# Token scale of the mixer heads on DVE, sparse heads spread over two products, reloads on POOL's queue

## The chip, the cores and the metric

The kernel runs on one core of a Trainium2 chip. The metric is the device time of one execution in microseconds (us), and a kernel's time is the median over its runs.

## The reference

One layer of a hybrid decoder block, for one sequence of 512 tokens with a width of 2048, all in f32. The part that matters here is the mixer: eight heads of forgetting attention (FoX, group A) and eight heads of sparse attention (NSA, group B), each group normalised over its 1024 columns, scaled, and multiplied with `w_out`:

```python
o_f = _fox_attention(fh(q_f), fh(k_f), fh(v_f), log_f)
o_n = _nsa_attention(nq(q_n), nkv(k_c), nkv(v_c), nkv(k_s), nkv(v_s), nkv(k_w), nkv(v_w),
                     gates, positions, cmp_pos, w_kc1, w_kc2, w_vc1, w_vc2)
y_f = _rmsnorm(o_f.reshape(B, S, FOX_HEADS * HEAD_DIM), beta_fox)
y_n = _rmsnorm(o_n.reshape(B, S, NSA_HEADS * HEAD_DIM), beta_nsa)
return jnp.concatenate([y_f, y_n], axis=-1) @ w_out
```

Ahead of it stand the modulation by `c @ w_ada`, a norm and the projection `u @ w_in`; behind it a residual, a second norm, a SwiGLU feed-forward layer and the final norm.

## The kernel before, in words

**Products.** Activations lie transposed, 128 columns by 512 tokens in a tile. Each f32 product is made of three matmuls on values cut to a high and a low half (high x high, low x high, high x low). `gemm` (L287) goes over the contraction in chunks of 256 rows: SP loads a raw chunk (L225, tag `wr`, 3 buffers), ACT copies the high half (L244), DVE subtracts to get the low half (L249), and PE multiplies. The halves have 2 buffers (`wh`, `wl`), and every third chunk uses a spare pair (`wx`).

**Order of work.** SP's queue is kept in the order in which the program is written (L109). In the attention stage the other engines' orders are made by the compiler's scheduler, in which what stands earlier in the program comes first where both are ready; from L1244 on all orders are as written. The attention runs as a list of steps (score, flip, value product) of which `gemm` takes some per chunk (`n_att`, L301). Other side work, the modulation blocks `side_ada` (L373) and the sparse heads' mixing `side_mix`, are generators advanced by `pump` (L365), some steps per chunk.

**Stage around the change.** A loop over four pairs of FoX heads (L986) makes q and k (L988) and then v (L999) of a pair, each with its own `gemm`, while attention steps of earlier heads run. v's product has 8 chunks of 24 matmuls of 256 columns. Each finished head is copied from PSUM (L864, tag `sc`), stored to DRAM (`osp`, L865, ACT's queue), squared (L871) and the square added on POOL (L875). When all eight heads of a group are there, the sums over columns (L882) give each token's scale 1/rms, which `rows_of` (L172) spreads into a tile of rows with 8 matmuls (L175) and a copy on ACT (L177): `rbn` for the sparse group, `rbf` for FoX.

**Mixing.** `reload` (L966) brings a head back from DRAM into a tile of tag `sc`, which has five buffers and which the attention's probabilities `p`, the head's copy `o` and its square `sq` use as well. `mix_chunk` (L959) multiplies it by the token scale (L960; on DVE for FoX heads 0, 2, 4, 6, on POOL for the rest), scales it by beta into the high half of `y` on ACT (L962), and makes the low half on DVE (L963).

**The sparse heads** are mixed by `mix_nsa` (L971): its first step makes `rbn`, each further step reloads and mixes one head (8 to 15). `mix_hook` (L982) pumps it in v's product of the last pair: one step in chunk 1, two in each chunk after, so that all heads are through with chunk 5. What might be left is pumped at L1023.

**`w_out`** follows (L1030). Its rows are taken in the order of `order`: heads 8 to 15 (sparse) first, then 0 to 7 (FoX). The first group `g0` has four banks and stops after the sparse heads (4 chunks of 512 columns, 24 matmuls of 512 columns each, L1031), with the last two FoX heads' attention beside it. Then the attention is drained (L1032), the FoX scale rows are made (L1033), and the second group `g1` (two banks, 4 chunks of 256 columns, 12 matmuls each, L1041) runs over the sparse heads, while `fox_hook` (L1036) reloads and mixes two FoX heads per chunk. The FoX halves of `g0` and `g1` come in the loop of L1205, then the remaining columns of `w_out`, with the residual (L1076), whose results POOL's queue stores (L1234).

Of the kernel before, what the change touches and what calls it, by code (L numbers as in the profile page):

```python
# [13 lines left out]
OP = mybir.AluOpType  # L14
# [9 lines left out]
FH = 8  # L24
# [55 lines left out]
def hymba_block(ctx: ExitStack, tc: tile.TileContext, x, c, positions, w_ada, b_ada, norm_attn,  # L80
                norm_ffn, w_in, b_fgate, cmp_pos, w_kc1, w_kc2, w_vc1, w_vc2, beta_fox, beta_nsa,
                w_out, w_gate, w_up, w_down, final_norm, cst, out):
    nc = tc.nc
# [18 lines left out]
    def uid(s):  # L102
        n_uid[0] += 1
        return f"{s}_{n_uid[0]}"
# [9 lines left out]
    def split_ap(t):  # L114
        return t.bitcast(F32)
# [56 lines left out]
    def rows_of(r, tag, s):  # L172
        b = bank(tag)
        for t in range(NT):
            nc.tensor.matmul(b[:, t * P:(t + 1) * P], r[:, t:t + 1].to_broadcast([P, P]), ident,  # L175
                             start=True, stop=True)
        nc.scalar.copy(s, b)  # L177
        return s
# [5 lines left out]
    for t in range(NT):  # L184
        for g in range(4):
            src = xtok[t, g // 2][:, g % 2, :]
# [30 lines left out]
    def load_w(parts, ct, nk=2, extra=None, src=None, width=T, bufs=3):  # L217
        return fetch_w(parts, ct, nk, extra, src, width, bufs)()
# [68 lines left out]
    def gemm(parts, a, nchunk, outs, extra=None, order=None, n_ada=0, n_cmp=0, n_att=0, k0=0, k1=None,  # L287
             hook=None, start=0, first=()):
        order = list(range(nchunk)) if order is None else order
        for ct in range(k0 // 2, (nchunk if k1 is None else k1) // 2):  # L290
            i = ct - k0 // 2
            wh, wl = first[i]() if i < len(first) else load_w(parts, order[2 * ct] // 2, extra=extra)
            pump(side_ada, n_ada)
            pump(side_cmp, n_cmp if ct > 1 else ct)
            pieces = [x for o in outs for x in bank_pieces(o)]
            for n, piece in enumerate(pieces):
                for k in range(2):
                    i = ct * 2 + k
                    piece(wh, wl, k, a[order[i]], i == start, i == nchunk - 1)
                if 2 * n + 2 in (len(pieces) - len(pieces) % 2, 2 * len(pieces)):  # L300
                    att.run(n_att)  # L301
            if hook is not None:
                hook(ct)
# [5 lines left out]
    def bank_pieces(out):  # L309
        kind, w0, n, b = out  # L310

        def ws(wh, wl, k, ahl, first, last):
            mm_ws(b, wh, wl, k, w0, *ahl, first, last)

        def tok(t):
            ts = slice(t * P, (t + 1) * P)

            def f(wh, wl, k, ahl, first, last):
                ah, al = ahl[0][:, ts], ahl[1][:, ts]
                if kind == "as":  # L320
                    mm_as(b[t][:, 0:n], wh[:, k, w0:w0 + n], wl[:, k, w0:w0 + n], ah, al, first, last)
                else:
                    pick = [v[:, k, 0:3 * P].rearrange("p (a b) -> p a b", b=P)[:, 0::2, :]
                            if kind == "as02" else v[:, k, w0:w0 + n] for v in (wh, wl)]
                    mm_as(b[t // 2][:, t % 2, :], pick[0], pick[1], ah, al,
                          first and t % 2 == 0, last, skip_group_check=True)
            return f

        return [ws] if kind == "ws" else [tok(t) for t in range(NT)]
# [35 lines left out]
    def pump(side, n):  # L365
        while n and side:
            try:
                next(side[0])
                n -= 1
            except StopIteration:  # L370
                side.pop(0)
# [31 lines left out]
    def act_tile(name, i):  # L403
        h = act.tile([P, T], F32R, tag="ah", name=uid(name + "h"), bufs=ND)
        l = act.tile([P, T], F32R, tag="al", name=uid(name + "l"), bufs=ND)
        return h, l
# [100 lines left out]
    while step < SLOTS + 8 or todo:  # L507
# [9 lines left out]
        i = {7: 0, 0: 1, 1: 2}.get(r, 3)  # L517
# [4 lines left out]
        i = AT.get(r, 3) if j < NJ else AT_END.get(r, 3)  # L522
# [44 lines left out]
        if n is not None:  # L567
            jj = n // 8
            for k2, sec in ((0, 1), (1, 0)):
                m0 = sec * ND + 2 * jj  # L570
                nc.vector.tensor_tensor(mod[:, m0:m0 + 2], sums[jj][:, 2 * k2:2 * k2 + 2], b_mod[:, m0:m0 + 2],
                                        op=OP.add)
# [38 lines left out]
    def sc_tile(name):  # L611
        return pa.tile([P, T], F32, tag="sc", name=uid(name), bufs=5)
# [45 lines left out]
    def q_tmp(name):  # L658
        return pa.tile([P, T], F32, tag="qh", name=uid(name), bufs=6)
# [144 lines left out]
    osp = dram.tile([FH + NH, P, T], F32, name="osp")  # L804
# [73 lines left out]
    def sum_rstd(tiles, n, tag, name, b=None):  # L878
        b = bank(tag) if b is None else b
        for i, a in enumerate(tiles):  # L880
            for t in range(NT):
                nc.tensor.matmul(b[:, t:t + 1], a[:, t * P:(t + 1) * P], one_col, start=i == 0 and t == 0,  # L882
                                 stop=i == len(tiles) - 1, skip_group_check=True)
        return rstd_of(b[:, 0:NT], n, name)
# [72 lines left out]
    y = {}  # L957

    def mix_chunk(src, i, rb):  # L959
        (nc.gpsimd if i >= FH or i % 2 else nc.vector).tensor_tensor(src, src, rb, op=OP.mult)  # L960
        h, l = act_tile("y", i)
        nc.scalar.activation(h, src, AF.Copy, scale=beta[:, i:i + 1])  # L962
        nc.vector.scalar_tensor_tensor(l, src, beta[:, i:i + 1], split_ap(h), op0=OP.mult, op1=OP.subtract)  # L963
        y[i] = (h, l)

    def reload(i):  # L966
        o = sc_tile("or")
        nc.sync.dma_start(o, osp[i])
        return o

    def mix_nsa():  # L971
        while "r" not in rs_n:
            yield
        rb = rows_of(rs_n["r"], "s", q_tmp("rbn"))
        yield
        for h in range(NH):
            mix_chunk(reload(8 + h), 8 + h, rb)
            yield

    side_mix = [mix_nsa()]  # L980

    def mix_hook(ct):  # L982
        if ct >= 1:
            pump(side_mix, 1 if ct == 1 else 2)

    for pr in range(4):  # L986
        Z = [bank("mm") for _ in range(4)]
# [4 lines left out]
        for i in range(2):  # L992
# [7 lines left out]
             hook=mix_hook if pr == 3 else None, first=w_vf)  # L1000
# [19 lines left out]

    while "r" not in rs_n:
        att.step()
    pump(side_mix, 1000)  # L1023

    def out_group(i0, n, tags):
        Z = [bank(t) for t in tags[:n]]
        return [cols(w_out, i0 * P, n * P)], y, ND, [("ws", m * P, P, Z[m]) for m in range(n)]

    order = list(range(8, 16)) + list(range(8))
    g0 = out_group(0, 4, BANKS_A)  # L1030
    gemm(*g0, order=order, n_ada=1, n_att=1.25, k1=8)  # L1031
    att.drain()  # L1032
    rb = rows_of(sum_rstd(osum[0], FH * HD, "o", "rsf"), "o", q_tmp("rbf"))  # L1033
    fox = order[8:]

    def fox_hook(ct):  # L1036
        for h in fox[2 * ct:2 * ct + 2]:
            mix_chunk(reload(h), h, rb)
# [239 lines left out]
    rb = ps2.tile([P, T], F32, tag="y", name=uid("py"), bufs=8)  # L1278
# [11 lines left out]
    for s in range(S):  # L1290
# [20 lines left out]
        n, i = divmod(s - A0, 4)  # L1311
# [66 lines left out]
    for p, ph in enumerate(phases):  # L1378
# [3 lines left out]
        for g in range(4):  # L1382
            Z = banks4()

            def hook(ct):
                if p == 0 and ct == 2:
                    for i in range(4 * g, 4 * g + 4):
                        nc.sync.dma_start(hT[i], hsd[i])
                if p == 3 and g == 3 and ct == 2:
                    fsum["b"] = bank("o")  # L1390
                    sum_tok(fsum, fsum["t"], True, False)
                if nxt and (ct % 2 or nk < 12):
                    b.append(h_tile(nxt.pop(0)))

            gemm([cols(w_down[P * ph[0]:], 512 * g, 512)], a, nk, [("ws", m * P, P, Z[m]) for m in range(4)],
                 hook=hook, first=w_first if p == 0 and g == 0 else ())
# [42 lines left out]
```

## Time and profile before

| what | value |
|---|---|
| median of 3 runs | 2440.64 us (2437.82 to 2442.27) |
| the profiled execution | 2438.08 us |
| its span, first to last instruction | 2436.3 us |
| mean granted clock of TensorE | 0.977 |
| busy share of PE, DVE, ACT, POOL | 96%, 65%, 42%, 14% |
| reloads of heads (L968) | 16 of 256 KB, from SP's queue |

PE is the matrix engine, DVE the vector engine, ACT the scalar engine, POOL the GpSimd engine; SP only sends transfers. A matmul's row shows a duration longer than the distance to the next, since matmuls are pipelined; the distances of the starts give the rate. The granted clock is a share of full speed: 1.00 is 2.4 GHz and 0.50 is 1.2 GHz. In a row of a timeline, what stands in brackets is the idle time of the engine just before and what ended it. In a row that merges several instructions (x2), the duration runs from the first one's start to the last one's end, waits between them included. SPq is SP's queue. A row of busy time by stretch has the stretch, its length, then the busy us and the instructions (x) of PE, of PE's weight loads, of DVE, ACT and POOL, then the granted clock, the busy share of the DMA engines and GB/s.

### The profile page before, as it was taken

Reading aid. Unit: us, or ns where it says so; the run is one execution under the profiler, and the core shown is the slowest. Engines: PE = TensorE matmul, PEld = TensorE weight load, DVE = VectorE, ACT = ScalarE, POOL = GpSimd, SP = SyncE. Lnnn points to the kernel's source line nnn. Section 1 sums busy time; section 2 is a strip of 40 time slices with the busy share of each in tenths; the row PEclk is TensorE's granted clock in tenths of the full one; section 3 lists DMA queues with packets and bytes.
Section 4 is the critical chain, followed back from the end, with each engine's and each line's share of the span. In section 5 each row is a group of like instructions: output and inputs, shape, how many; then the busy total and the mean of one; then the engine's idle time right before and its main releaser. Section 6 shows DMA issues by size and latency. Waiting matters only on the chain.

```text
span 2436.3 us, 38417 instructions
## 1 busy us (share of the span) xinstructions
PE 2349.1 (96%) x14677; PEld 2100.5 (86%) x14677; DVE 1583.2 (65%) x2719; ACT 1026.5 (42%) x1544; POOL 341.2 (14%) x370
## 2 busy tenths in 40 slices
PE   6998999999999999889999999999999999999998
PEld 4777887888887777789999999999999888888887
DVE  7867887787655566596777677777676633333333
ACT  3335444334323323365555555555555422222233
POOL 0002002000102021251222221212121100000010
PEclk8999999999999999899999999999999999999998
DMA  9974643453563287469898889988988644333322
GB/s 331 322 232 143 178 142 101 122 180 119 164 181 122 82 274 255 159 145 231 214 230 220 221 217 229 224 219 219 216 200 196 187 156 141 121 117 122 105 94 99
DMA packets 322713, 440.31 MB, mean 181 GB/s; under 512 B 26224, under 2 KB 217552, under 8 KB 322528
## 3 DMA queue, kind: packets, MB, share of 16 engines
q1 hardware_dynamic: 289104, 348.21, 44.3%
q0 software_dynamic: 31120, 85.45, 18.9%
q10 hardware_dynamic: 2304, 4.20, 0.5%
q8 instruction: 115, 1.88, 0.3%
q14 instruction: 70, 0.57, 0.1%
HBM read 340.18 MB, written 28.38 MB: 151 GB/s over the span
## 4 chain that ended last, share of the span: by engine, by line
PE 55%; DVE 1%; DMA 0%; issue 0%; ACT 0%; SPq 0%; DVEq 0%; ACTq 0%
PE py L1173 12%; PE py L1176 11%; PE py L1175 11%; PE psmm L278 3%; PE psmm L280 3%; PE psmm L279 3%; PE pss L278 2%; PE pss L279 2%; PE pss L280 2%; PE pso L278 1%; PE pso L279 1%; PE pso L280 1%; DMA wr<-in_w_down_dram 0%; PE pso L1070 0%; DVE ul L1153 0%
## 5 line engine op out<-in xcount | busy, mean ns | idle before, releaser
L249 DVE TENSOR_TENSOR wl<-wr,wh 128x1024 fp32r<-128x1024 f32 (+2 forms) x211 | 238.8, 1132 | 371.1 <-ACT wh L244 369.5
L244 ACT CAST wh<-wr 128x1024 fp32r<-128x1024 f32 (+2 forms) x211 | 199.7, 948 | 528.9 <-PE psmm L279 204.0
L1176 PE MATMUL py<-uh,ls 128*128 128x256 f32 x1408 | 398.4, 283 | 2.8 <-DVE ls L1119 2.8
L1173 PE MATMUL py<-uh,hs 128*128 128x256 f32 x1408 | 399.3, 284 | 0.9 <-DVE ev L1190 0.5
L1175 PE MATMUL py<-ul,hs 128*128 128x256 f32 x1408 | 398.4, 283 | 1.8 <-DVE ul L1153 1.8
L1113 ACT CAST hs<-sum 128x1024 fp32r<-128x1024 f32 x176 | 184.6, 1049 | 377.0 <-PE py L1175 256.6
L1119 DVE TENSOR_TENSOR ls<-sum,hs 128x1024 fp32r<-128x1024 f32 x176 | 215.3, 1223 | 196.3 <-ACT hs L1113 196.3
L1175 PE MATMUL py<-ul,hx 128*128 128x256 f32 x1056 | 298.7, 283 | 4.1 <-DVE ul L1153 4.1
L1173 PE MATMUL py<-uh,hx 128*128 128x256 f32 x1056 | 299.3, 283 | 1.7 <-ACT uh L1152 1.4
L1176 PE MATMUL py<-uh,lx 128*128 128x256 f32 x1056 | 298.3, 282 | 0.0
L1176 PEld LDWEIGHTS py<-uh,ls 128*128 128x128 f32 x1408 | 268.0, 190 | 3.6 <-DVE ls L1119 3.6
L1173 PEld LDWEIGHTS py<-uh,hs 128*128 128x128 f32 x1408 | 268.1, 190 | 2.7 <-DVE ev L1190 1.3
L1175 PEld LDWEIGHTS py<-ul,hs 128*128 128x128 f32 x1408 | 268.0, 190 | 2.7 <-DVE ul L1153 2.7
L1109 POOL DMA_DIRECT2D lx<-raw x176 | 156.1, 887 | 579.2 <-ACT lx L1108 431.8
L1175 PEld LDWEIGHTS py<-ul,hx 128*128 128x128 f32 x1056 | 200.8, 190 | 4.9 <-DVE ul L1153 4.8
L1173 PEld LDWEIGHTS py<-uh,hx 128*128 128x128 f32 x1056 | 200.6, 190 | 2.2 <-ACT uh L1152 1.7
L1176 PEld LDWEIGHTS py<-uh,lx 128*128 128x128 f32 x1056 | 200.6, 190 | 0.0
L386 DVE SCALAR_TENSOR_TENSOR acc<-ad,sl,acc 128x512 f32<-128x512 f32 x180 | 143.2, 796 | 41.7 <-DMA ad<-in_w_ada_dram 40.1
L1108 ACT ACTIVATE lx<-raw 128x768 fp32r<-128x768 f32 x176 | 148.0, 841 | 1.8 <-DMA raw<-in_w_gate_dram 1.8
L1104 ACT CAST hx<-raw 128x768 fp32r<-128x768 f32 x176 | 144.4, 820 | 9.0 <-DMA raw<-in_w_gate_dram 9.0
L278 PE MATMUL psmm<-fh,wh 128*128 128x512 f32 x352 | 137.0, 389 | 0.0
L280 PE MATMUL psmm<-fh,wl 128*128 128x512 f32 x352 | 136.9, 389 | 0.0
(442 smaller groups left out, 5290.4 us busy)
## 6 DMA issues: line engine op xcount, KB each, us to landing
lx<-raw POOLq DMA_DIRECT2D x176, 384.0 KB, 5.2
ad<-in_w_ada_dram SPq DMA_DIRECT2D x128, 512.0 KB, 3.9
raw<-in_w_up_dram SPq DMA_DIRECT2D x176, 256.0 KB, 4.1
raw<-in_w_gate_dram SPq DMA_DIRECT2D x176, 256.0 KB, 4.4
wr<-in_w_down_dram SPq DMA_DIRECT2D x88, 512.0 KB, 3.7
ad<-in_w_ada_dram SPq DMA_DIRECT2D x128, 256.0 KB, 6.0
wr<-in_w_in_dram SPq DMA_DIRECT2D x104, 256.0 KB, 3.4
wr<-in_w_in_dram SPq DMA_DIRECT2D x24, 512.0 KB, 4.9
```

The costliest lines, as they stand in the source:

```text
L244: nc.scalar.copy(wh[:, :, sc], v)
L249: nc.vector.tensor_tensor(held[1][:, :, sc], v, split_ap(held[0])[:, :, sc], op=OP.subtract)
L278: nc.tensor.matmul(dst, wh[:, k, w], ah, start=first, stop=False)
L279: nc.tensor.matmul(dst, wh[:, k, w], al, start=False, stop=False)
L280: nc.tensor.matmul(dst, wl[:, k, w], ah, start=False, stop=last)
L1108: nc.scalar.activation(lx[s], raw[s][:, 1:4, :], AF.Copy, scale=-1.0)
L1109: nc.gpsimd.dma_start(split_ap(lx[s]), raw[s][:, 1:4, :], accum_op=OP.add)
L1113: nc.scalar.copy(hs[s], sums[s])
L1119: nc.vector.tensor_tensor(ls[s], sums[s], split_ap(hs[s]), op=OP.subtract)
L1173: nc.tensor.matmul(o, wh[:, wi, js], vh[:, vi, :], start=k == 0 and j == 0, stop=False, skip_group_check=True)
L1175: nc.tensor.matmul(o, wh[:, wi, js], vl[:, vi, :], start=False, stop=False, skip_group_check=True)
L1176: nc.tensor.matmul(o, wl[:, wi, js], vh[:, vi, :], start=False, stop=k == KG - 1, skip_group_check=True)
```

## The change

All token-scale multiplies go to DVE. The reloads are issued on POOL's queue instead of SP's. In v's product of the last pair each chunk from the second on takes one step of the sparse mixing (rows in chunk 1, heads 8 to 13 in chunks 2 to 7), head 14 follows behind the loop, and head 15 goes into the first chunk of `w_out`'s first group; `while len(y) < 2` has nothing to do there, and the later chunks' pumps find the generator ended.

```diff
@@ -957,7 +957,7 @@
     def mix_chunk(src, i, rb):
-        (nc.gpsimd if i >= FH or i % 2 else nc.vector).tensor_tensor(src, src, rb, op=OP.mult)
+        nc.vector.tensor_tensor(src, src, rb, op=OP.mult)
         h, l = act_tile("y", i)
@@ -965,7 +965,7 @@
     def reload(i):
         o = sc_tile("or")
-        nc.sync.dma_start(o, osp[i])
+        nc.gpsimd.dma_start(o, osp[i])
         return o
@@ -981,7 +981,7 @@
     def mix_hook(ct):
         if ct >= 1:
-            pump(side_mix, 1 if ct == 1 else 2)
+            pump(side_mix, 1)
@@ -1020,7 +1020,9 @@
     while "r" not in rs_n:
         att.step()
-    pump(side_mix, 1000)
+    pump(side_mix, 1)
+    while len(y) < 2:
+        pump(side_mix, 1)
@@ -1028,7 +1030,7 @@
     g0 = out_group(0, 4, BANKS_A)
-    gemm(*g0, order=order, n_ada=1, n_att=1.25, k1=8)
+    gemm(*g0, order=order, n_ada=1, n_att=1.25, k1=8, hook=lambda ct: pump(side_mix, 2 if ct < 2 else 1000))
     att.drain()
```

## Rows read from the trace of the kernel before

**Rows 1.** The page, part 1: busy time and share of the span, TensorE

```profile
PE 2349.1 (96%) x14677; PEld 2100.5 (86%) x14677; DVE 1583.2 (65%) x2719; ACT 1026.5 (42%) x1544; POOL 341.2 (14%) x370
```

**Rows 2.** Busy time by stretch, 771 to 880 us

```profile
771.00:803.00 32.00, 27.16 (x212) 26.65 (x211) 18.22 (x20) 13.29 (x20) 12.67 (x8) 0.95 0.37 116
803.00:840.00 37.00, 37.00 (x178) 29.17 (x177) 17.77 (x45) 12.37 (x31) 1.30 (x1) 1.00 0.13 43
840.00:860.00 20.00, 16.70 (x69) 12.50 (x68) 13.18 (x20) 10.05 (x16) 6.48 (x4) 0.83 0.51 173
860.00:880.00 20.00, 20.00 (x89) 16.13 (x88) 12.56 (x16) 5.16 (x7) 0.39 (x1) 1.00 0.71 236
```

**Rows 3.** Timeline of PE, value product of the last head pair (start, duration)

```profile
786.94 0.28 PE L284 MATMUL psmm<-wh,ul 128*128 128x256 f32 x1
787.06 0.28 PE L285 MATMUL psmm<-wl,uh 128*128 128x256 f32 x1
790.05 0.39 PE L283 MATMUL psmm<-wh,uh 128*128 128x256 f32 x1 [2.71 <-ACT wh L244]
...
792.68 0.58 PE L285 MATMUL psmm<-wl,uh 128*128 128x256 f32 x1 [2.13 <-DVE wl L249]
...
795.61 0.28 PE L283 MATMUL psmm<-wh,uh 128*128 128x256 f32 x1
...
802.45 0.40 PE L278 MATMUL psmm<-yh,wh 128*128 128x512 f32 x1
```

**Rows 4.** Timeline of SP's queue, reloads (L968) and weight loads (L225)

```profile
767.40 15.45 SPq L968 DMA_DIRECT2D or<-osp  x2
782.90 0.43 SPq L225 DMA_DIRECT2D wr<-in_w_in_dram  x1
...
831.96 1.95 SPq L968 DMA_DIRECT2D or<-osp  x2
834.00 0.39 SPq L225 DMA_DIRECT2D wr<-in_w_out_dram  x1
...
843.67 7.61 SPq L968 DMA_DIRECT2D or<-osp  x2
```

**Rows 5.** SP's waits, 735 to 880 us: total, times, longest

```profile
SPq L968 <- PE pss L841: 32.5, 3, 28.9
SPq L968 <- DVE yl L963: 24.0, 5, 14.6
```

**Rows 6.** Timeline of PE, end of the attention and w_out's second group

```profile
842.88 0.40 PE L280 MATMUL pss<-yh,wx 128*128 128x512 f32 x1
844.16 2.04 PE L175 MATMUL pso<-cs,rsfr 128*128 128x128 f32 x8 [0.89 <-DVE rsfr L169]
845.86 0.77 PE L278 MATMUL pss<-yh,wh 128*128 128x512 f32 x1
...
859.57 0.50 PE L278 MATMUL psmm<-yh,wh 128*128 128x512 f32 x1
```

**Rows 7.** Timeline of ACT, second weight chunk of w_out's second group

```profile
843.04 0.60 ACT L244 CAST wh<-wr 128x512 fp32r<-128x512 f32 x1
```

**Rows 8.** The tile or: duration ns min/median/max, first and last start

```profile
L960 POOL TENSOR_TENSOR or<-or,rbn x8: 1286/1710/1756, 779.4 to 790.4; 128x512 f32<-128x512 f32 x8
L960 DVE TENSOR_TENSOR or<-or,rbf x4: 680/1233/1776, 846.9 to 857.3; 128x512 f32<-128x512 f32 x4
```

**Rows 9.** Line 963 (low halves of y), 770 to 800 us, the same columns

```profile
L963 DVE SCALAR_TENSOR_TENSOR yl<-or,vec,yh x8: 736/1432/1460, 781.5 to 793.2; 128x512 fp32r<-128x512 f32 x8
```

**Rows 10.** DMA issues: KB each, median us from issue to landing

```profile
or<-osp SPq DMA_DIRECT2D x16, 256.0 KB, 2.9
```

**Rows 11.** Line 1234 (POOL's transfers to DRAM): durations of the issue, landing times

```profile
L1234 POOL DMA_DIRECT2D hsd<-hT x16: 539/557/632, 879.6 to 1017.3; - x16
...
DMA to landing us min/median/max: 2.3/3.0/5.4
```

**Rows 12.** Stretch after the sparse group's column sums, columns as in rows 2

```profile
591.00:592.00 1.00, 1.00 (x5) 1.00 (x6) 0.79 (x4) 0.99 (x2) 0.00 (x0) 0.50 0.08 30
```

## The prediction, made before the changed kernel was run

> **What bounds the kernel now.** I read the page first: TensorE (PE) is busy 96% of the span [rows 1]; only what PE loses can be won back. Next the busy time by stretch around the edit, 771 to 880 us [rows 2]: 803 to 840 is full at full clock, as is 860 to 880, while 771 to 803 and 840 to 860 hold gaps (27.16 of 32 us and 16.70 of 20 us busy) and a granted clock of 0.95 and 0.83, that is, part of each ran at the lower level, 1.2 GHz instead of 2.4. Two stalls, then, both in the stage that the change touches. The timelines of PE give their size, that of SP's queue their cause.
>
> Stall one, in the value product of the last FoX pair. Its matmuls start 0.12 us apart. Chunk 4 ends with the start at 787.06; chunk 5 starts at 790.05 after a wait for its weights' high half, and goes on at 792.68 after a wait for the low half; until 795.61 the clock is at half [rows 3]. From 787.06 to 795.61 there are 16 steps, 16 x 0.12 = 1.92 us at full speed; 8.55 us passed. **Lost: 6.6 us.** Cause: SP sends in written order, and two reloads of sparse heads hold it from 767.40 for 15.45 us; the weight load behind them goes at 782.90 [rows 4]. The second of the two waited for a buffer: there are five of tag "sc", five reloads hold them, and the first is freed by the first head's low half (line 963) [rows 5], which starts at 781.5 [rows 9].
>
> Stall two, in w_out's second group (4 chunks x 2 banks x 2 x 3 = 48 matmuls). The first chunk's 12 end with the start at 842.88; the other 36 run until 859.57, with the 8 matmuls of the FoX scale rows ahead of them [rows 6]. At full speed a 512-column matmul takes 20 us / 88 = 0.227 us (88 weight loads, 860 to 880 us [rows 2]), so 36 x 0.227 + 8 x 0.12 = 9.1 us; from 843.11 (842.88 + 0.23) to 859.57 it took 16.5. **Lost: 7.3 us**, of which the half clock is 3.4 (0.17 x 20 us [rows 2]) and waiting the rest. Cause: SP stands at a FoX reload for 28.9 us, until the last attention head gives a buffer back [rows 5]; the second chunk's load goes only at 834.00 [rows 4] and its copy on ACT comes at 843.04 [rows 7], when PE has run out of other work. The fourth chunk's load stands behind 7.61 us more of reloads [rows 4].
>
> **The change, part by part.**
> *Reloads to POOL's queue.* 16 issues leave SP; with them go its waits for buffers, 32.5 + 24.0 us in all [rows 5]. SP then holds only weight and modulation loads, each waiting for one of three raw buffers, which turn over with PE. In stall one the load now sent at 782.90 follows the low half of chunk 2, some ten us earlier; in stall two all four chunks can be in SBUF before 830. On POOL, 16 issues cost 0.56 us each [rows 11], 9 us together; queued behind a waiting reload there is only the sum-of-squares add (line 875), at most one head's. POOL is busy 14% [rows 1] and loses twelve multiplies of about 1.7 us [rows 8], so this I cost at nothing; the cover is POOL's idle time, and without it, it is 9 us. Landing is 3.0 us where POOL sends 256 KB to DRAM [rows 11], 2.9 for these reloads from SP [rows 10]: no charge. No row shows a load from DRAM on POOL here; the bounds are nothing and 2.5 us more per reload (the slowest of line 1234's, 5.4 [rows 11], less 2.9).
>
> DVE operations with two SBUF inputs are slow beside POOL's multiplies: line 963 has a median of 1.43 us there and a minimum of 0.74 [rows 9]. The Trainium skill, page "SBUF — State Buffer", section "Who interferes with whom", says why: such a DVE instruction and a GpSimd one that reads SBUF exclude each other; here the trace agrees. But the same page speaks against this change: its section "SBUF: two separate sides" warns that transfers issued from GpSimd starve while DVE holds the shared port pair, and advises the SP or ACT queue. By the rows so far (3.0 against 2.9 us) it costs nothing; by the page it is the last rival below.
>
> *Multiplies to DVE.* Eight sparse and four FoX multiplies more, 12 x 0.68 us (the uncontended minimum [rows 8]) = 8.2 us on DVE. Given back: up to 8 x 0.7 = 5.6 us on the sparse low halves [rows 9] and some 3 on the FoX ones and the multiplies already there (up to 1.78 us [rows 8]). Net between -0.4 and +8.2; I take nothing, being nearest to the contended rows. It is off the path while DVE has room: 18.22 of 32 us and 13.18 of 20 [rows 2]. DVE now waits for the scale rows and for reloads, which POOL did before; behind it queue the weights' low halves, for which PE waits. The copied weights have two chunks of lead (2 x 2.9 us), so a delay of one head (0.68 + 0.74 us) doesn't reach PE.
>
> *One head per step.* Heads 8 to 13 in the value product, 14 after it, 15 in w_out's first chunk. Head 8 is ready at the same time (its scale rows come at 779.4 [rows 8]); w_out wants heads 14 and 15 only in its fourth chunk, over 15 us (3 chunks x 24 x 0.227) after it starts. Cost: nothing, covered by those three chunks; without them, one head, 1.4 us.
>
> **Sum.** Stall one: -6.6 (bounds 0 and -6.6; the whole, since the load's only other wait is a raw buffer). Stall two: between 0 and -7.3. Its waits, 3.9, should go, as the weights are there as filler. The half clock, 3.4, I leave in: after the sparse group's column sums the clock also stood at 0.50 [rows 12], and these sums stay. So -3.9. Total -10.5, from the profiled execution's 2438.08 (a span of 2436.3 and 1.8 around it) to 2427.6. The median of the runs shown is 2.6 higher: 2440.64 - 10.5 = 2430.1, forecast **2430 us**. What is late next is the FoX chain: column sums, scale rows, then the multiplies; nothing here shortens it.
>
> **Rivals.**
> 1. *Only stall one goes.* ACT's copy of the second chunk stays behind the FoX square root in ACT's order, though its load is early. 2440.64 - 6.6 = 2434. For it: that copy now comes late in ACT's order [rows 7]. Against: ACT copies other chunks ahead of attention work as soon as they are in.
> 2. *The stall moves.* POOL's reloads wait for the same five buffers, or the order comes out otherwise; DVE waits instead of SP, and PE with it. Or the change does not act: the loads were held by raw buffers. 2440, within 4.9 us. Against: SP's waits name the sc buffers [rows 5].
> 3. *Slower: DVE becomes the bound.* Place: the last product and w_out's second group. The added multiplies stand ahead of the weights' low halves and nothing is given back: 12 x 0.68 = 8.2 us on the path, 2449. It decides once DVE's work fills the stretch: in the second, 13.2 + 2.7 us against the 12.7 that would be left of 20. Against: half of the FoX mixing can run in 860 to 880, where DVE is busy 12.56 of 20 [rows 2].
> 4. *POOL's reloads come late.* The last three FoX reloads wait for a buffer each, and DVE waits for each in turn: 3 x 2.5 = 7.5 us back, 2438. The page named above would have it so; the landing times of POOL's other transfers [rows 11] mostly speak against it.
>
> **How the numbers follow.** Forecast 0.55; its own range is 2426.7 (all of 13.9) to 2433. Rival 1 0.20, rival 2 0.11, rival 3 0.08, rival 4 0.06. A measurement here tells some 0.2%, 4.9 us, from no change. Faster by more: the forecast and nearly all of rival 1, 0.74. Within it: rival 2, most of rival 4 and the rest of rival 1, 0.18. Slower: 0.08. Range 2425 to 2438.5: the forecast and rival 1 whole, rival 4 and part of 2, leaving out rival 3.
>
> **What would show it.** Right: on SP's queue no reload, and the value product's sixth load before 778.6 us; PE without a wait for lines 244 or 249 from 771 until w_out starts near 796; the second chunk of the second group copied before the FoX square root; line 963 near 0.74 us throughout. The clock after the column sums tells whether the 3.4 us stay. Wrong: PE waiting for line 249 while DVE sits in line 960, DVE waiting for reloads from POOL over 3 us long, or the sum-of-squares add standing behind a reload so that the column sums come late.

## The result, and the profile after

The changed kernel takes **2426.24 us** (median of 6 runs, 2423.31 to 2431.53) against 2439.51 us before (6 runs): a ratio of 0.9947, 95% interval 0.9936 to 0.9958, so 13 us less. 2430 was forecast, with a range of 2425 to 2438.5 and 0.74 on faster by over 0.2%.

Busy time of the changed kernel by stretch (columns as in [rows 2]):

```profile
771.00:803.00 32.00, 32.00 (x224) 29.34 (x222) 21.56 (x37) 14.30 (x24) 1.61 (x3) 1.00 0.42 132
803.00:840.00 37.00, 37.00 (x188) 30.01 (x188) 19.49 (x49) 17.53 (x35) 4.42 (x7) 1.00 0.34 114
840.00:860.00 20.00, 18.39 (x78) 14.14 (x77) 13.63 (x20) 5.88 (x8) 1.18 (x3) 1.00 0.62 211
860.00:880.00 20.00, 15.76 (x64) 11.66 (x63) 14.49 (x18) 4.81 (x8) 6.19 (x7) 0.97 0.76 247
```

771 to 840 is now full at full clock. The gaps have moved behind 840: 18.39 and 15.76 of 20 us, where [rows 2] show 16.70 and 20.00. POOL, 12.67 us busy in the first stretch before, is down to 1.61.

Timeline of SP's queue, changed kernel: no reload is left between the loads, and the value product's are all sent by 774.77 (743.79 + 30.98), where [rows 4] have one at 782.90:

```profile
743.79 30.98 SPq L225 DMA_DIRECT2D wr<-in_w_in_dram  x8
779.17 36.94 SPq L225 DMA_DIRECT2D wr<-in_w_out_dram  x9
```

The changed kernel's groups of one line each: multiplies (L960), low halves (L963), reloads (L968) and their landing (durations in ns: min/median/max, first and last start):

```profile
L960 DVE TENSOR_TENSOR or<-or,rbn x8: 679/682/691, 774.7 to 803.3; 128x512 f32<-128x512 f32 x8
...
L963 DVE SCALAR_TENSOR_TENSOR yl<-or,vec,yh x16: 740/744/751, 776.5 to 847.3; 128x512 fp32r<-128x512 f32 x16
...
L968 POOL DMA_DIRECT2D or<-osp x16: 536/536/607, 740.9 to 840.9; - x16
...
DMA to landing us min/median/max: 2.7/3.0/5.3
```

The low halves take 0.74 us throughout, where [rows 9] have a median of 1.43; all 16 reloads land in 3.0 us at the median, 0.1 more than from SP [rows 10].

Timeline of PE, changed kernel, at the place of stall two:

```profile
831.55 0.40 PE L280 MATMUL pss<-yh,wx 128*128 128x512 f32 x1
831.78 0.40 PE L278 MATMUL pss<-yh,wh 128*128 128x512 f32 x1
...
834.76 1.05 PE L175 MATMUL pso<-cs,rsfr 128*128 128x128 f32 x8
835.57 0.48 PE L279 MATMUL pss<-yl,wh 128*128 128x512 f32 x1
...
840.90 0.39 PE L278 MATMUL psmm<-yh,wh 128*128 128x512 f32 x1
```

Timeline of ACT, changed kernel: the copy of the second chunk, at 843.04 in [rows 7], and the FoX square root:

```profile
824.75 0.62 ACT L244 CAST wh<-wr 128x512 fp32r<-128x512 f32 x1 [1.17 <-PE psmm L279]
...
831.61 0.20 ACT L164 ACTIVATE rsfs<-rsf 128x4 f32<-128x4 f32 x1 [0.95 <-DVE rsf L163]
```

The copy comes before the square root (831.61), PE goes from the first chunk's weights (`wx`, 831.55) straight on to the second's (`wh`, 831.78) while the scale rows are made, and the second group ends at 840.90: 9.35 us from 831.55, where [rows 6] show 16.69.

**Where the time went.** The profiled spans differ by 11.5 us (2436.3 and 2424.8), but not only in the changed part: the scale rows' first matmul starts at 777.66 before and 772.96 after, although no edit touches the work of PE up to there, and from the second norm to the end the two executions differ by 2.9 us the other way. The start of the scale rows scatters as widely over the other profiles (772.3 to 779.2), so I compare lengths of stages between fixed points of the timelines: the value product (sparse scale rows' first matmul to the first matmul on `y`), first group (to the first FoX column sum), second group (to the first matmul on a FoX half of `y`), and late part (to the second norm's L163). "Stretch" below is the first three together: 81.9 us before, 67.9 after. Two executions, one of the kernel before (11492 us) and one of e2 (7941 us), stood out by a factor of three or more and are left out of the ratios.

| kernel | reloads | multiplies | sparse heads | value product | first group | second group | late part | ratio (95%) |
|---|---|---|---|---|---|---|---|---|
| before | SP | POOL, DVE | two a chunk | 24.79 | 38.33 | 18.79 | 159.3 | 1 |
| after | POOL | DVE | one a chunk | 18.16 | 38.34 | 11.44 | 163.6 | 0.9947 (0.9936 to 0.9958) |
| e1 | POOL | POOL, DVE | two | 21.51 | 38.33 | 11.45 | 165.1 | 0.9978 (0.9967 to 0.9989) |
| e2 | SP | POOL, DVE | one | 20.30 | 43.32 | 19.11 | 158.9 | 1.0000 (0.9987 to 1.0014) |
| e3 | SP | DVE | two | 18.62 | 38.33 | 16.24 | 163.0 | 0.9961 (0.9947 to 0.9975) |
| e4 | SP | DVE | one | 18.16 | 44.99 | 16.12 | 161.4 | 0.9996 (0.9987 to 1.0005) |
| e5 | POOL | POOL, DVE | one | 22.91 | 38.34 | 11.44 | 164.9 | 0.9971 (0.9959 to 0.9982) |
| e8 | POOL | DVE | two | 18.55 | 38.26 | 11.44 | 164.9 | 0.9947 (0.9929 to 0.9965) |
| e7, below | POOL | DVE | one a chunk | 18.97 | 39.26 | 11.65 | 157.6 | 0.9916 (0.9899 to 0.9933) |

Stall one is gone whole (24.79 - 18.16 = 6.6 us), stall two whole (18.79 - 11.44 = 7.35 us), and 4.3 us come back in the late part: -9.7 us by stages; with -4.7 ahead and +2.9 behind that makes the pair's -11.5. Over the table the stages agree with the ratio within a us in e1, e2 and e4, but give 3 to 7 us less than measured in the changed kernel, e3, e5, e8 and e7 (9.7 against 13 in the changed kernel). That rest lies in stretches that no edit touches, and I did not settle it.

### The profile page after: what moved, and what is told of

It is laid out like the page before. It is cut to its first block, busy times and chain, and to the rows that moved or that the text cites. A ratio compares the mean times of both kernels' runs of the same rounds, so it can differ in the third digit from the quotient of the medians.

```text
span 2424.8 us, 38417 instructions
## 1 busy us (share of the span) xinstructions
PE 2340.7 (97%) x14677; PEld 2092.8 (86%) x14677; DVE 1580.6 (65%) x2731; ACT 1027.1 (42%) x1544; POOL 331.5 (14%) x374
## 4 chain that ended last, share of the span: by engine, by line
PE 55%; DVE 1%; DMA 0%; issue 0%; ACT 0%; SPq 0%; DVEq 0%; ACTq 0%
PE py L1175 12%; PE py L1178 12%; PE py L1177 12%; PE psmm L278 3%; PE psmm L280 3%; PE psmm L279 3%; PE pss L278 2%; PE pss L279 2%; PE pss L280 2%; PE pso L280 1%; PE pso L278 1%; PE pso L279 1%; DMA wr<-in_w_down_dram 0%; PE pso L1072 0%; DVE ul L1155 0%
## 5 line engine op out<-in xcount | busy, mean ns | idle before, releaser
L249 DVE TENSOR_TENSOR wl<-wr,wh 128x1024 fp32r<-128x1024 f32 (+2 forms) x211 | 238.0, 1128 | 371.9 <-ACT wh L244 365.5
L244 ACT CAST wh<-wr 128x1024 fp32r<-128x1024 f32 (+2 forms) x211 | 199.7, 948 | 528.0 <-PE psmm L279 203.2
```

Of the source, the lines that this page charges most:

```text
L244: nc.scalar.copy(wh[:, :, sc], v)
L249: nc.vector.tensor_tensor(held[1][:, :, sc], v, split_ap(held[0])[:, :, sc], op=OP.subtract)
```

## Experiments

**e1: the reloads alone.**

```diff
-        nc.sync.dma_start(o, osp[i])
+        nc.gpsimd.dma_start(o, osp[i])
```

> Only the reloads move to POOL's queue; multiplies and spreading stay as before. Measured beside the total: the stretch from PE's first matmul of the sparse scale rows to its first matmul on a FoX half of y (81.9 us before, 67.9 after the whole change). Theory A, SP standing at reloads is the cause of both stalls: the stretch falls to 68 to 70 us, the time by 10 to 14 us. Theory B, the spreading takes stall one and the reloads' queue only stall two: 74 to 75 us, the time by about 7. Theory C, POOL's own multiplies now stand ahead of the later reloads in its queue and hold DVE and PE up: 71 us or more with PE waiting in the value product or the second group.

Measured: 0.9978, some 5 us; stretch 71.3 us. Stall two goes whole, but of stall one only 3.3 us: theory C's bound of 71 holds. SP sends the value product's last five loads without a reload between them, and PE still waits. SP's timeline in e1:

```profile
763.24 17.78 SPq L225 DMA_DIRECT2D wr<-in_w_in_dram  x5
```

ACT's timeline in e1: high halves of heads (L962) and copies of weights (L244):

```profile
...
788.63 0.72 ACT L962 ACTIVATE yh<-or,vec 128x512 fp32r<-128x512 f32 x1 [0.98 <-POOL or L960]
789.26 0.60 ACT L244 CAST wh<-wr 128x512 fp32r<-128x512 f32 x1
```

DVE's timeline in e1: low halves of heads (L963) and of weights (L249):

```profile
787.69 1.46 DVE L963 SCALAR_TENSOR_TENSOR yl<-or,vec,yh 128x512 fp32r<-128x512 f32 x1 [0.25 <-ACT yh L962]
789.39 0.75 DVE L963 SCALAR_TENSOR_TENSOR yl<-or,vec,yh 128x512 fp32r<-128x512 f32 x1 [0.24 <-ACT yh L962]
790.06 0.68 DVE L249 TENSOR_TENSOR wl<-wr,wh 128x512 fp32r<-128x512 f32 x1
```

POOL's timeline in e1, the multiplies:

```profile
780.95 7.65 POOL L960 TENSOR_TENSOR or<-or,rbn 128x512 f32<-128x512 f32 x5 [17.22 <-ACT rbn L177]
```

The loads were all sent by 781.02 (763.24 + 17.78), yet chunk 5's copy (789.26) is the next thing ACT does after five heads' high halves, which wait for POOL 0.5 to 1.4 us each; and its low half (790.06) stands behind the heads' low halves, which take up to 1.46 us. POOL takes 7.65 us for five heads, and this pace sets when the weights are copied. What theory C named is seen too, but later: POOL sends the last three reloads only from 788.55, behind its multiplies, and PE waits once more, 0.50 and 0.38 us at 797.08 and 797.96, for copies that stand behind these three heads. The same order stood in the kernel before: chunk 5's load goes at 782.90 [rows 4], but its copy comes only here in ACT's timeline of before, behind six high halves (the first at 780.73):

```profile
...
788.77 0.72 ACT L962 ACTIVATE yh<-or,vec 128x512 fp32r<-128x512 f32 x1 [0.95 <-POOL or L960]
789.39 0.60 ACT L244 CAST wh<-wr 128x512 fp32r<-128x512 f32 x1
```

**e2: the spreading alone.**

```diff
-            pump(side_mix, 1 if ct == 1 else 2)
+            pump(side_mix, 1)
-    pump(side_mix, 1000)
+    pump(side_mix, 1)
+    while len(y) < 2:
+        pump(side_mix, 1)
-    gemm(*g0, ...
+    gemm(*g0, ..., hook=lambda ct: pump(side_mix, 2 if ct < 2 else 1000))
```

> Only the spreading (one sparse head per chunk); reloads on SP, multiplies as before. The first five reloads find buffers and the sixth is now issued behind the value product's last weight load. Theory A in its narrow form (any reload on SP costs): the stretch stays near 82 us and the time the same. Theory B (it is only what stands behind the sixth reload that counts): stall one goes, stall two stays, the stretch is 75 us and the time falls by 5 to 8 us.

Measured: 1.0000, no change; stretch 82.7. Theory A's numbers are met, but not for its reason, and theory B misses. The value product does shorten, by 4.5 us (20.30), and on SP's timeline of e2 the reloads of its eight sparse heads now stand singly between the loads but for one pair, at 779.51; but w_out's first group takes 5.0 us more, which neither foresaw, and stall two stays.

**e3: the multiplies alone.**

```diff
-        (nc.gpsimd if i >= FH or i % 2 else nc.vector).tensor_tensor(src, src, rb, op=OP.mult)
+        nc.vector.tensor_tensor(src, src, rb, op=OP.mult)
```

> Only the multiplies move to DVE. Theories A and B: the buffer of the first sparse head comes free about as early, SP stands at the same two places, the stretch is 80 to 82.5 us and the time within 2 us of before. Theory C (contention of POOL and DVE is a cause): the low halves fall from 1.43 to 0.74 us and the stretch by 3 us or more.

Measured: 0.9961, some 10 us; stretch 73.2, 8.7 less than before. Theories A and B fall, C holds. SP's timeline in e3:

```profile
764.22 14.87 SPq L968 DMA_DIRECT2D or<-osp  x2
779.14 0.43 SPq L225 DMA_DIRECT2D wr<-in_w_in_dram  x1
```

ACT's timeline in e3:

```profile
776.91 1.95 ACT L962 ACTIVATE yh<-or,vec 128x512 fp32r<-128x512 f32 x3 [0.76 <-DVE or L960]
780.70 1.39 ACT L962 ACTIVATE yh<-or,vec 128x512 fp32r<-128x512 f32 x2 [1.84 <-DVE or L960]
782.30 0.73 ACT L962 ACTIVATE yh<-or,vec 128x512 fp32r<-128x512 f32 x1 [0.20 <-DVE or L960]
782.93 0.61 ACT L244 CAST wh<-wr 128x512 fp32r<-128x512 f32 x1
```

DVE's timeline in e3:

```profile
782.12 2.07 DVE L963 SCALAR_TENSOR_TENSOR yl<-or,vec,yh 128x512 fp32r<-128x512 f32 x3
784.11 0.69 DVE L249 TENSOR_TENSOR wl<-wr,wh 128x512 fp32r<-128x512 f32 x1
```

SP stands at the reloads for 14.87 us, nearly as long as before (15.45), and sends chunk 5's load behind them, at 779.14. Yet the copy comes at 782.93, 3.8 us after the load, where 6.5 us passed before (782.90 to 789.39), because the heads ahead of it on ACT no longer wait for POOL; and three low halves of heads take 2.07 us together. Against the changed kernel the value product loses only 0.46 us (18.62 - 18.16) of the 6.6. So SP's stand alone was not what stall one cost. The edit takes away two things at once, POOL's pace and the slow low halves beside POOL; which of them is worth how much was not taken apart.

The second group stays 4.8 us longer than in the changed kernel (16.24 against 11.44). PE's timeline in e3 there:

```profile
834.80 1.25 PE L175 MATMUL pso<-cs,rsfr 128*128 128x128 f32 x8 [0.88 <-DVE rsfr L169]
...
841.85 0.50 PE L280 MATMUL pss<-yh,wl 128*128 128x512 f32 x1 [0.66 <-DVE wl L249]
```

Busy time of e3 around this wait:

```profile
831.00:834.00 3.00, 2.92 (x21) 2.24 (x19) 0.34 (x3) 2.03 (x4) 0.00 (x0) 1.00 0.23 87
...
836.00:838.00 2.00, 2.00 (x7) 1.52 (x6) 1.30 (x3) 1.16 (x2) 0.00 (x0) 0.50 0.55 170
838.00:840.00 2.00, 2.00 (x8) 1.58 (x7) 2.00 (x4) 1.89 (x4) 0.00 (x0) 0.73 0.00 0
```

PE waits 0.88 us for the scale rows (0.89 in [rows 6]), and the clock falls to 0.50. In the changed kernel there is other work for PE here, and it stays at 1.00.

**e4: the change with its reloads on SP.**

```diff
-        nc.gpsimd.dma_start(o, osp[i])
+        nc.sync.dma_start(o, osp[i])
```

> The changed kernel with its reloads back on SP. Theory A narrow: both stalls are back, stretch 81 to 83 us. Theory B: stall one stays away by the spreading, stall two is back with its half clock, stretch 75 us, time 5 to 8 us below before and about 7 above the changed kernel.

Measured: 0.9996, no change; stretch 79.3. Neither theory holds: of B, stall one does stay away, but the time does not fall. The value product is as short as after the whole change (18.16), but the first group takes 44.99 us and the second 16.12. Two waits in e4's first group (timeline of PE):

```profile
806.29 0.64 PE L841 MATMUL pss<-cs,p 128*128 128x128 f32 x2 [1.53 <-DVE p L830]
...
811.88 0.80 PE L278 MATMUL psmm<-yh,wx 128*128 128x512 f32 x1 [1.19 <-ACT wx L244]
```

Busy time of e4 in two stretches there:

```profile
796.00:806.00 10.00, 8.75 (x43) 6.84 (x42) 4.40 (x13) 2.10 (x7) 0.00 (x0) 1.00 0.05 17
806.00:816.00 10.00, 8.52 (x23) 6.20 (x24) 7.74 (x17) 5.78 (x12) 0.00 (x0) 0.52 0.08 26
```

An attention matmul (L841) waits for DVE, w_out's second chunk waits for its copy, and for about ten us PE runs at 0.52. This group takes 38.3 us with the reloads on POOL (e7, with its added block, apart), and with them on SP where the heads are not spread (before, e3). So spreading with reloads on SP makes a new stall larger than the spreading is worth. No transfer is late here: in e4 head 15's reload goes at 788.33 and the last of the next three loads of w_out at 793.2, and all of them land within 5.0 us; but ACT copies the second chunk only at 810.80, next behind head 15's high half (810.17), where the changed kernel copies it at 788.48. It is the order that came out; why it came out so was not taken apart.

**e5: the change with its multiplies as before.**

```diff
-        nc.vector.tensor_tensor(src, src, rb, op=OP.mult)
+        (nc.gpsimd if i >= FH or i % 2 else nc.vector).tensor_tensor(src, src, rb, op=OP.mult)
```

> The changed kernel with its sparse multiplies and half of its FoX ones back on POOL. What the first runs left: the stretch falls apart into the value product (from the sparse scale rows to w_out's first matmul: 24.8 us before, 18.2 after), w_out's first group (to the FoX column sums: 38.3 and 38.3) and the second group (to its end: 18.8 and 11.4). Theory P, ACT and DVE keep their order, so the weights' copies stand behind heads that POOL's multiplies pace at 1.7 us each: the value product takes 19.5 to 22 us, the other two 38.3 and 11.5, the time is 2 to 5 us above the changed kernel. Theory Q, with spreading and early loads POOL's pace no longer matters: 18.2 us and the same time.

Measured: 0.9971, some 6 us above the changed kernel by the ratios; value product 22.91, a little over the bound, the other two as expected. Theory P, with more lost than it said: POOL itself waits 2.05 and 0.92 us for reloads that it sent only from 784.77 on, behind its multiplies. The wait in e5's PE timeline is for the copies again:

```profile
793.22 0.39 PE L283 MATMUL psmm<-wh,uh 128*128 128x256 f32 x1 [2.01 <-ACT wh L244]
...
794.10 0.39 PE L285 MATMUL psmm<-wl,uh 128*128 128x256 f32 x1 [0.38 <-DVE wl L249]
```

**e8: the change without the spreading.**

```diff
-            pump(side_mix, 1)
+            pump(side_mix, 1 if ct == 1 else 2)
-    pump(side_mix, 1)
-    while len(y) < 2:
-        pump(side_mix, 1)
+    pump(side_mix, 1000)
-    gemm(*g0, ..., hook=lambda ct: pump(side_mix, 2 if ct < 2 else 1000))
+    gemm(*g0, ...)
```

> The changed kernel without the spreading (two sparse heads per chunk as before). Theory P: multiplies on DVE and early loads are enough, the spreading gives nothing: value product 18.0 to 18.8 us, first group 38.3, second 11.4, time within 2 us of the changed kernel. Theory S, the spreading keeps DVE clear for the weights' low halves: value product 20 us or more, time 2 us or more above the changed kernel.

Measured: 0.9947, the same as the whole change; value product 18.55 against 18.16. Theory P: the spreading is worth some 0.4 us of the value product here and nothing that shows in the time.

**e7: a version that beats both.** What comes back in the late part is idle time of PE. Busy time over the late part of the changed kernel:

```profile
840.90:1004.50 163.60, 153.22 (x673) 122.26 (x671) 99.33 (x123) 46.76 (x60) 30.12 (x34) 0.99 0.74 242
```

The same of the kernel before:

```profile
859.57:1018.90 159.33, 153.13 (x673) 123.94 (x672) 96.29 (x117) 45.37 (x58) 29.70 (x33) 0.98 0.76 249
```

PE idles 10.4 us there after (163.60 - 153.22) and 6.2 before (159.33 - 153.13). Its waits from 841 to 880 in the changed kernel are all for the copied halves of w_out's weights (timeline of PE):

```profile
849.88 0.50 PE L280 MATMUL psmm<-yh,wl 128*128 128x512 f32 x1 [1.56 <-DVE wl L249]
...
869.71 0.50 PE L280 MATMUL pss<-yh,wl 128*128 128x512 f32 x1 [1.11 <-DVE wl L249]
...
872.75 0.50 PE L278 MATMUL pss<-yh,wh 128*128 128x512 f32 x1 [0.48 <-ACT wh L244]
...
878.69 0.62 PE L278 MATMUL pss<-yh,wh 128*128 128x512 f32 x1 [2.65 <-ACT wh L244]
```

They have different causes. The chunk of the first wait was copied at 839.31, but its low half stood on DVE behind the low halves of the FoX heads (DVE's timeline, changed kernel):

```profile
845.96 2.07 DVE L963 SCALAR_TENSOR_TENSOR yl<-or,vec,yh 128x512 fp32r<-128x512 f32 x3
...
848.61 1.22 DVE L249 TENSOR_TENSOR wl<-wr,wh 128x1024 fp32r<-128x1024 f32 x1
```

At the last one, ACT had waited 5.33 us for the transfer before it copied the chunk at 878.02.

The edit moves one modulation block (8 loads and their 16 multiply-adds on DVE) out of the late part into w_out's first group, where the DMA engines are 0.34 busy in the changed kernel (803 to 840). It also keeps the last value product free of the blocks' loads, as it is in the changed kernel, and takes their steps out of the FoX half of w_out's second group:

```diff
-    side_ada.extend(ada_block(pa, sec, j) for sec, j in todo_ada[:9])
+    side_ada.extend(ada_block(pa, sec, j) for sec, j in todo_ada[:10])
-        gemm(p_vf, ..., n_ada=1, ...
+        gemm(p_vf, ..., n_ada=1 if pr < 3 else 0, ...
-    gemm(*g0, ..., n_ada=1, ...
+    gemm(*g0, ..., n_ada=2, ...
-    side_ada.extend(ada_block(pf, sec, j) for sec, j in todo_ada[9:])
+    side_ada.extend(ada_block(pf, sec, j) for sec, j in todo_ada[10:])
-        gemm(*g, order=order, k0=k0, hook=x_hook, n_ada=1)
+        gemm(*g, order=order, k0=k0, hook=x_hook, n_ada=0 if i0 == 4 else 1)
```

> The changed kernel with one modulation block (8 loads of 512 KB and their 16 multiply-adds) moved from w_out's later groups into its first group, and none of their steps in the second half of the two-bank group, where loads are waited for. In the changed kernel the part from the end of the second group's sparse half to the second norm's column sums takes 163.6 us against 159.3 before, so about 4 us are given back there. Theory T, that part is bound by transfers: it falls to 155 to 160 us, the first group stays within 1 us of 38.3, the time is 3 to 7 us below the changed kernel. Theory U, it is bound by DVE's and ACT's order: 162 us or more; or the block's loads hold the first group's weights up and it takes 40 us or more: same or slower.

Measured: **2421.3 us** median, a ratio of **0.9916 (0.9899 to 0.9933)** to before: some 7.5 us under the changed kernel by the ratios, whose intervals do not overlap, and 5 by the medians. The late part takes 157.6 us, 6 less than after, the first group 39.26 and the value product 18.97. Theory T by its numbers. Busy time of e7 where the changed kernel had 18.39 and 15.76, and over its late part, where PE idles 5.5 us (157.62 - 152.14):

```profile
840.00:860.00 20.00, 19.08 (x83) 14.85 (x82) 17.29 (x25) 7.97 (x12) 1.61 (x3) 1.00 0.58 190
860.00:880.00 20.00, 19.89 (x88) 16.12 (x87) 10.05 (x13) 6.92 (x10) 5.99 (x7) 1.00 0.79 267
845.48:1003.10 157.62, 152.14 (x665) 122.76 (x663) 84.82 (x106) 46.64 (x60) 30.29 (x34) 0.98 0.70 225
```

Waits of ACT for w_out's transfers from 840 to 1005 us (total, times, longest), the changed kernel and then e7:

```profile
ACT wh L244 <- DMA wr<-in_w_out_dram: 58.5, 16, 6.6
...
ACT wh L244 <- DMA wr<-in_w_out_dram: 23.7, 6, 5.8
```

The block took DVE's work with it as well: DVE is busy 84.82 us in e7's late part, 99.33 in the changed kernel's. So e7 shows where time was to be had, but not whether the loads or DVE's multiply-adds held PE up; and its edits were not tried one by one.

## Why the prediction was right, and where it was not

*The two stalls and their sizes*: right. 6.6 and 7.3 us were read off PE's timeline as lost, and 6.6 and 7.35 us came back. The stage was read rightly: what a stall is worth shows where PE stands still, whatever ends it.

*Stall one's cause ("two reloads of sparse heads hold it")*: wrong as the whole cause. I took the late load as the whole cause, because SP's 15.45 us ended where the load began. e3 leaves that stand as it was and keeps 0.46 us of the stall; e1 takes it away and keeps half. The load was late, but the copies stood behind heads that POOL's multiplies paced, and [rows 3] held a sign of it: PE's second wait there, 2.13 us, is for line 249, DVE's low half. Of the 6.6 us the reloads alone bring 3.3 (e1), the spreading alone 4.5 (e2), the multiplies alone 6.2 (e3), reloads and multiplies together 6.2 (e8); but reloads and spreading with the multiplies left on POOL only 1.9 (e5). The worths of the parts do not add up.

*Multiplies to DVE, "I take nothing"*: the step that failed in size. By themselves they bring 6.2 us in the value product and 2.6 in the second group. I netted DVE's busy time and found room; what counted was that ACT and DVE keep their order, and a head took 1.7 us on POOL against 0.68 on DVE while the weights' copies stood behind it. The bounds I gave, -0.4 to +8.2 us of DVE work, held no gain on the path beyond 0.4. Nor does the trace quite agree that the two engines exclude each other: both are slowed, the low half from 0.74 to 1.43 us [rows 9] and POOL's multiply from 1.29 to 1.71 [rows 8], but such a pair takes 1.7 us per head, less than the 2.0 of one after the other (1.29 + 0.74).

*Reloads cost nothing on POOL*: right. 16 issues of 0.54 us, landing in 3.0 us, and DVE waited 0.6 us once for one. The Trainium skill's page "SBUF — State Buffer", section "SBUF: two separate sides", had warned of transfers starved while DVE runs an operation in a 2-port mode. None shows here: the reloads landed in 2.7 to 5.3 us. My rival 4 had stretched the warning to any work of DVE, and it is out.

*Stall two's cause*: right. With nothing but the reloads taken off SP (e1) the second group falls from 18.79 to 11.45 us.

*Stall two, "the half clock I leave in"*: wrong by 3.4 us. The column sums are the same matmuls as before, and the clock stays at 1.00 through 803 to 860 in the changed kernel; in e3, where PE waits 0.88 us behind them, it falls. The sums of [rows 12] had come behind a wait as well, 0.75 us before their start at 589.05. So the sums alone, to which I put down [rows 12], did not take the clock here, and with other work for PE behind them the whole 7.35 us came back.

*One head per step, cost nothing*: right for this change (e8), but only with the reloads on POOL: with them on SP the first group grows by 5.0 to 6.7 us (e2, e4).

*What is late next*: the FoX chain, as I had it, only in part. Its multiplies and low halves on DVE hold up PE's first wait of the late part, 1.56 us; the later waits, for w_out's weights, come when that work is over. I charged nothing for this part, and it is 4.3 us longer in the profiled pair, 4.3 to 5.8 in the four kernels with a second group of 11.4. Two errors, +3.4 us missed and 4.3 us not charged, cancel in the total; 2430 was near for that reason too, and some 3 us of the measured 13 are those left open above. e7 shows that these 4 us can be had back.

*Rivals*: 1 fell with the copy at 824.75, 2 with both stalls gone, 3 with a DVE that is 21.56 of 32 us busy in the first stretch and keeps PE waiting nowhere in the three changed stages.

## What to carry to other kernels

An engine that keeps its order passes its slowest partner's pace on: before blaming a late load, look at what stands ahead of the copy on the copying engine, and whom that waits for. An off-path engine's 1.7 us operation can cost PE more than 0.68 us on a busier engine. And time won in one stage can be lost in the next dense one, so look for a stretch where the DMA engines are idle, and DVE has room, to move side work into.

## What the runs showed that was not expected

The granted clock did not fall after 16 one-column matmuls when ordinary matmuls followed without a gap (1.00 from 803 to 860 in the changed kernel); it fell to 0.50 in e3, where PE also waited 0.88 us behind them. And executions of programs with the same order up to a point reached that point up to 6.9 us apart (772.3 us in e8, 779.2 in e1), half of what the whole change brings: single profiles had to be compared stage by stage.
